# A hybrid decoder block on one core: scans with one SBUF operand, carries left in place, fused state and gate operations, ordered loads in the down stage

## The chip, the cores and the metric

The kernel runs on one core of a Trainium2 chip. The metric is the device time of one execution in microseconds (us). The time before is the median of three runs. The core's engines are TensorE (PE, matmuls and transposes; PEld is its weight load), VectorE (DVE), ScalarE (ACT), GpSimd (POOL) and SyncE (SP), whose queue issues most of the DMAs.

## The reference

One decoder layer for 2048 tokens of width 1024, in float32. A projection feeds three token mixers that work side by side:

```
q, k = rms_norm(q), rms_norm(k)                     # stick-breaking attention, 6 heads of 64
z = q @ k.T * scale                                 # keys s < query t only
A[t, s] = sigmoid(z[t, s]) * prod_{s<j<t} (1 - sigmoid(z[t, j]))
o_b = rms_norm(A @ v)                               # per head
S_t = diag(exp(log_f_t)) S_{t-1} + k_t^T v_t        # GLA (4 heads, 48 x 96), HGRN2 (4 heads, 128 x 64)
o_t = q_t S_t                                       # then rms_norm per head, times silu(gate)
x = x + concat(o_a, o_b, o_c) @ w_out               # the Out stage
gate, up = rms_norm(x) @ w_ffn_up                   # d_ff = 2816
x = x + (silu(gate) * up) @ w_ffn_down
```

The product over j is a running product from right to left, so 1 - sigmoid(z) = sigmoid(-z) is scanned along the keys from the newest to the oldest.

## The kernel before

The work runs in stages: projections (0 to 755 us of the trace), mixers (755 to 1592, from 1425 on mixed with the first tiles of Out), Out alone (1592 to 1782), the FFN's up half (to 2639) and its down half (to 3146). Matmuls in float32 are done as three matmuls on high and low parts (names ending in h and l): a high part is a rounding on ScalarE (L248), a low part a subtraction on DVE or POOL (L249). A scheduler puts the instructions of each engine, and the DMAs on SP's queue, in the order of an estimate of its own; `tc.keep_in_program_order` holds an instruction behind the one written before it on its engine or queue. In the mixers the order of PE is written out by hand (`Chain`).

**Stick-breaking.** A unit is one head, a group of 512 queries and a chunk of 512 keys: 60 units, each in four slots of 128 queries (`z_step`). A slot makes z (128 queries x up to 512 keys) in one of two PSUM banks, kp = sigmoid(-z) and w = sigmoid(z) on ScalarE into SBUF, then the scan on DVE (L993). The scan reads kp twice: as its data and as a second operand that the operation `bypass` ignores. Its result pr has one column more than keys; the leftmost, the product over the whole chunk, is copied by POOL into a carry tile (L996) for the next older chunk of the same head. Last, w times the shifted pr (L997), mostly on POOL. Then w is transposed by PE (`t_step`) and multiplied with v (`a_step`).

**The recurrences.** `hg_chunk` and `gla_chunk` update their states s_h and s_g 15 times each: POOL multiplies by the decay (L1192, L1247), DVE adds the new part from PSUM (L1193, L1248).

**Out.** Sixteen tiles of 128 tokens. `load` takes the mixers' output m, sums squares per head (14 ScalarE squares, L826), forms the inverse roots and multiplies m by them (three on DVE, L834) and by the gates (three on POOL). `turn` transposes m by PE into a PSUM bank (mt, L849) and splits it. 48 matmuls (po) a tile add the product with w_out. `norm` squares and scales the sum for the FFN (L857, L860); `left` transposes it through the same single bank (xt, L867) and copies it out (xa, L869), and `left_sums` stores operands of the seven products of a Strassen scheme to `xs_s`.

**Up.** `left_in` loads them and splits them into SBUF tiles (ah, al) that stay for all 22 steps of a half. These tiles' region on the right side of SBUF is that of Out's pools and of the output weights woh and wol, which close before.

**Down.** Seven products, in the order 1, 2, 5, 6, 3, 7, 4, each with 11 k's of 24 matmuls (8 PSUM banks, three matmuls each): 1848. For each k, `left_dn` loads one or two left tiles (ar, xa; 512 KB) from `hs_s`, which up has written, and `right_dn` weights (br, xb; 256 KB); products 5, 6, 3 and 4 go on from the tiles xa and xb of an earlier product. After the third k of product 1 the 16 tiles of acc (the residual) are loaded in program order. After a product `flush_dn` adds its eight banks to acc; for products 5 and 7 ScalarE copies the bank to tmp (L1528) and POOL adds that to a second part (L245). Finished parts of acc are stored to the output after products 2, 3, 7 and 4.

Of the kernel before, what the change touches and what calls it, by code (L numbers as in the profile page):

```python
# [14 lines left out]
ALU = mybir.AluOpType  # L15
# [47 lines left out]
def hybrid_block(ctx: ExitStack, tc: tile.TileContext, x, norm_mix_g, w_in, gla_w_decay,  # L63
# [740 lines left out]
    class Out:  # L804
        def open(self):
# [5 lines left out]
            self.pt = open_pool(self.st, "d_pt", 1, PSUM, side="right")  # L811

        def load(self, t):
# [15 lines left out]
            dve.tensor_scalar(ms[:, 4:14], ms[:, 4:14], 1.0 / SD, EPS, op0=ALU.mult,  # L829
                              op1=ALU.add)  # L830
# [13 lines left out]
        def turn(self, prep, hf):  # L844
            t, m, _, mh, ml = prep
            pt = self.pt.tile([P, 4, P], F32, tag="pt", name=f"mt{t}_{hf}")
# [15 lines left out]
        def left(self, t, xt, kh):  # L862

            pt = self.pt.tile([P, KH, P], F32, tag="pt", name=f"xt{t}_{kh}")
# [61 lines left out]
    with ExitStack() as ph:  # L926
# [16 lines left out]
        kps = [sbk.tile([P, 513], F32, name=f"kp{i}", bufs=1) for i in range(NKP)]  # L943
        for t_ in kps:
            pool.memset(t_[:, 512:513], 1.0)
# [13 lines left out]
        def z_step(u, b):  # L959
            h, g, c = u.h, u.g, u.c  # L960
            if b == 0:
                if u.diag:
                    u.q = sio.tile([P, 2, 512], F32, tag="sq", name=f"sq{h}_{g}", bufs=3)
                    for s in range(2):
# [3 lines left out]
                    u.carry = [sbk.tile([P, 1], F32, tag=f"ca{i}", name=f"ca{h}_{g}_{i}", bufs=4)  # L968
                               for i in range(4)]
                else:  # L970
                    p = units[u.i - 2]
                    u.q, u.carry = p.q, p.carry
# [22 lines left out]
            if c > 0:  # L995
                pool.tensor_copy(u.carry[b], pr[:, 0:1])  # L996
# [597 lines left out]
```

## Time and profile before

| | before |
|---|---|
| median of three runs | 3143.91 us (3139.87 to 3149.15) |
| profiled execution | 3147.62 us |
| span of its trace | 3145.8 us |
| PE busy | 2831.5 us (90%) |
| DVE busy | 2116.2 us (67%) |
| ACT busy | 1344.4 us (43%) |
| POOL busy | 1639.2 us (52%) |

The span goes from the first to the last instruction of the profiled execution. The busy shares are means over stages that differ in what limits them, so the windows by stage have to be read for each part of the change.

### The profile page before, as it was taken

How to read it: one execution, taken by the hardware profiler on the slowest of the kernel's cores; microseconds unless marked ns; L12 is line 12 of the kernel's file. 1: busy time of each engine (PE TensorE's matmuls, PEld its weight loads, DVE VectorE, ACT ScalarE, POOL GpSimd, SP SyncE). 2: the span in 40 equal slices, each digit the busy share in tenths (PEclk: the TensorE clock that was granted, in tenths of full speed). 3: DMA queues.
4: the chain of work that ended last, by engine and by line, in shares of the span. 5: the costliest groups of instructions: out<-in, count | busy, mean ns of one | idle time of the engine just before them, and what ended most of it. 6: DMA issues, size and time to landing. Idle time of an engine off the chain costs nothing. (4 is left out here: it accounts for less than half of the span.)

```text
span 3145.8 us, 43879 instructions
## 1 busy us (share of the span) xinstructions
PE 2831.5 (90%) x14882; PEld 2309.9 (73%) x14882; DVE 2116.2 (67%) x3508; ACT 1344.4 (43%) x2834; POOL 1639.2 (52%) x1640
## 2 busy tenths in 40 slices
PE   5898999997888889878888799999999997899998
PEld 5897878996666666655666588888788885677776
DVE  8886665886888888988866455555755553267443
ACT  5554534453555555566644333333433332323222
POOL 5342554344787887854633244444544442257635
PEclk9999999998889998989988899999999998999999
DMA  3534432536533333123354332222422225564173
GB/s 116 159 108 134 139 127 97 136 94 166 153 104 107 98 100 93 58 94 108 130 173 161 134 114 85 87 87 84 142 87 81 81 81 216 212 234 144 64 241 131
DMA packets 346095, 389.82 MB, mean 124 GB/s; under 512 B 59152, under 2 KB 258064, under 8 KB 344080
## 3 DMA queue, kind: packets, MB, share of 16 engines
q1 hardware_dynamic: 341776, 381.77, 38.4%
q0 software_dynamic: 4096, 5.25, 0.5%
q8 instruction: 119, 1.95, 0.3%
q14 instruction: 104, 0.85, 0.1%
HBM read 278.93 MB, written 108.00 MB: 123 GB/s over the span
## 5 line engine op out<-in xcount | busy, mean ns | idle before, releaser
L1390 PE MATMUL gu<-ah,uh 128*128 128x512 f32 x1232 | 481.3, 391 | 10.1 <-ACT ah L248 10.1
L1391 PE MATMUL gu<-al,uh 128*128 128x512 f32 x1232 | 481.8, 391 | 6.0 <-DVE al L249 5.9
L1392 PE MATMUL gu<-ah,ul 128*128 128x512 f32 x1232 | 481.0, 390 | 0.0
L249 POOL TENSOR_TENSOR ul<-bs,uh 128x512 fp32r<-128x512 f32 x176 | 241.6, 1374 | 243.2 <-ACT uh L248 243.2
L249 POOL TENSOR_TENSOR ul<-us,uh 128x512 fp32r<-128x512 f32 x132 | 176.6, 1339 | 203.6 <-ACT uh L248 203.6
L1390 PEld LDWEIGHTS gu<-ah,uh 128*128 128x128 f32 x1232 | 232.3, 189 | 60.3 <-ACT ah L248 12.0
L1391 PEld LDWEIGHTS gu<-al,uh 128*128 128x128 f32 x1232 | 232.5, 189 | 56.9 <-DVE al L249 8.7
L1552 PE MATMUL dn<-dbh,dah 128*128 128x512 f32 x616 | 224.6, 402 | 48.4 <-ACT dbh L248 41.8
L1392 PEld LDWEIGHTS gu<-ah,ul 128*128 128x128 f32 x1232 | 232.3, 189 | 48.1
L245 DVE TENSOR_TENSOR h<-h,gu 128x512 f32<-128x512 f32 x176 | 120.9, 687 | 205.3 <-PE gu L1392 123.5
L1553 PE MATMUL dn<-dbl,dah 128*128 128x512 f32 x616 | 243.9, 396 | 12.7 <-POOL dbl L249 12.6
L1554 PE MATMUL dn<-dbh,dal 128*128 128x512 f32 x616 | 242.4, 395 | 3.1 <-DVE dal L249 3.0
L248 ACT ACTIVATE uh<-bs 128x512 fp32r<-128x512 f32 x176 | 110.9, 632 | 299.8 <-PE gu L1391 299.6
L993 DVE TENSOR_TENSOR_SCAN pr<-kp,ca 128x513 f32<-128x513 f32 x144 | 213.2, 1484 | 22.0 <-ACT kp L990 17.7
L997 POOL TENSOR_TENSOR w<-w,pr 128x512 f32<-128x512 f32 (+1 forms) x174 | 191.8, 1102 | 46.0 <-DVE pr L993 26.0
L990 ACT ACTIVATE kp<-z 128x512 f32<-128x512 f32 (+1 forms) x240 | 128.0, 533 | 183.4 <-PE z L104 168.7
L104 PE MATMUL z<-sk,sq 128*128 128x512 f32 (+1 forms) x480 | 170.7, 440 | 14.5 <-ACT w L991 8.1
L107 PE MATMUL wt<-ident,w 128*128 128x128 f32 x816 | 147.9, 294 | 39.2 <-POOL w L997 34.3
L1552 PEld LDWEIGHTS dn<-dbh,dah 128*128 128x128 f32 x616 | 118.4, 194 | 80.5 <-ACT dbh L248 49.3
L249 DVE TENSOR_TENSOR dal<-ar,dah 128x1024 fp32r<-128x1024 f32 x44 | 65.0, 1485 | 163.1 <-ACT dah L248 163.0
L248 ACT ACTIVATE uh<-us 128x512 fp32r<-128x512 f32 x132 | 83.1, 631 | 193.0 <-PE gu L1391 130.6
L104 PEld LDWEIGHTS z<-sk,sq 128*128 128x128 f32 x480 | 80.7, 208 | 104.7 <-issue 37.9
(385 smaller groups left out, 7845.1 us busy)
## 6 DMA issues: line engine op xcount, KB each, us to landing
us<-in_w_ffn_up SPq DMA_DIRECT2D x88, 512.0 KB, 3.8
ar<-hs_s SPq DMA_DIRECT2D x88, 512.0 KB, 4.0
hs_s<-h SPq DMA_DIRECT2D x44, 512.0 KB, 2.6
br<-in_w_ffn_down SPq DMA_DIRECT2D x88, 256.0 KB, 3.2
sk<-sk_s SPq DMA_DIRECT2D x60, 256.0 KB, 2.9
st<-xs_s SPq DMA_DIRECT2D x14, 1024.0 KB, 5.2
xt<-in_x SPq DMA_DIRECT2D x24, 512.0 KB, 4.8
sq<-sq_s SPq DMA_DIRECT2D x48, 256.0 KB, 4.8
```

What stands on the lines that cost most here:

```text
L104: self._add(nc.tensor.matmul(*a, **k))
L107: self._add(nc.tensor.transpose(*a, **k))
L248: act.activation(wh, st, AF.Copy)
L249: eng.tensor_tensor(wl, st, wh.bitcast(F32), op=ALU.subtract)
L993: dve.tensor_tensor_scan(pr[:, n::-1], kr, kr, 1.0 if u.diag else u.carry[b], op0=ALU.mult, op1=ALU.bypass)
L997: (dve if (b in DVE_B0 if g == 0 else b == DVE_B) else pool).tensor_tensor(w, w, pr[:, 1:n + 1], op=ALU.mult)
L1390: pe.matmul(pv, bh[:, k, :], ah[:, :, k, :], start=(k == 0), stop=False)
L1391: pe.matmul(pv, bh[:, k, :], al[:, :, k, :], start=False, stop=False)
L1392: pe.matmul(pv, bl[:, k, :], ah[:, :, k, :], start=False, stop=(k == KH - 1))
L1552: pe.matmul(pss[i], ah[:, ts_], bh, start=(k == 0), stop=False)
L1553: pe.matmul(pss[i], ah[:, ts_], bl, start=False, stop=False)
L1554: pe.matmul(pss[i], al[:, ts_], bh, start=False, stop=(k == NK - 1))
```

## The change

1. `z_step`: the scan's second operand, which `bypass` ignores, is a broadcast column of z in PSUM in place of kp. The results pr go to two fixed buffers of 529 columns, each slot at an offset `at` of its own, so that the leftmost column stays unharmed until the next chunk reads it as its carry; the POOL copies go. Where DVE multiplies, the second sigmoid is written over z in PSUM, and the product reads it there.
2. `hg_chunk`, `gla_chunk`: a multiplication and an addition become four, or two, fused operations on DVE that read the new part from PSUM.
3. `Out.load`: one ScalarE square of the whole tile and three DVE sums replace 14 squares; 14 fused DVE products replace three products on DVE and three on POOL.
4. Out has three more PSUM banks for its transposes once the mixers have closed theirs.
5. Up: the ah and al tiles of the first half are allocated in the reversed order of the products.
6. Down: all loads in program order, raw weight tiles in three buffers, the products in the order 1, 5, 6, 2, 3, 7, 4, both additions of products 5 and 7 by DVE from PSUM, and product 6's 16 POOL additions put off, two to each k of the next product.

```diff
@@ Out.load
+            sq = self.wk.tile([P, D], F32, tag="sq", name=f"msq{t}", bufs=1)
+            act.activation(sq, m, AF.Square)
             for a, b, w, i, j in segs:
-                for h in range(j - i):
-                    sj = self.sm.tile([P, GDV], BF16, tag="sj", name=f"sj{t}_{i}_{h}", bufs=1)
-                    act.activation(sj[:, :w], m[:, a + h * w:a + (h + 1) * w], AF.Square,
-                                   accum_out=ms[:, i + h:i + h + 1])
+                dve.tensor_reduce(ms[:, i:j], sq[:, a:b].rearrange("p (h d) -> p h d", d=w),
+                                  axis=AX.X, op=ALU.add)
...
             for a, b, w, i, j in segs:
-                mv = m[:, a:b].rearrange("p (h d) -> p h d", d=w)
-                dve.tensor_tensor(mv, mv, rs[:, i:j].unsqueeze(2).to_broadcast([P, j - i, w]),
-                                  op=ALU.mult)
-            pool.tensor_tensor(m[:, 0:384], m[:, 0:384], gt[:, 0:384], op=ALU.mult)
-            pool.tensor_tensor(m[:, 768:], m[:, 768:], gt[:, 384:], op=ALU.mult)
-            mv = m[:, 384:768].rearrange("p (h d) -> p h d", d=SD)
-            pool.tensor_tensor(mv, mv, gs64.unsqueeze(1).to_broadcast([P, SH, SD]), op=ALU.mult)
+                for n in range(i, j):
+                    cs = slice(a + (n - i) * w, a + (n - i + 1) * w)
+                    g_ = gt[:, cs] if a == 0 else gs64 if a == 384 else \
+                        gt[:, 384 + (n - i) * w:384 + (n - i + 1) * w]
+                    dve.scalar_tensor_tensor(m[:, cs], m[:, cs], rs[:, n:n + 1], g_,
+                                             op0=ALU.mult, op1=ALU.mult)
@@ z_step
-            pr = sbk.tile([P, 513], F32, tag="pr", name=f"pr{h}_{g}_{c}_{b}")
+            at = 4 * (g - c) + 2 * u.j + b // 2
+            pr = prs[b % 2][:, at:at + 513]
             act.activation(kp[:, :n], z, AF.Sigmoid, scale=-1.0)
-            act.activation(w, z, AF.Sigmoid)
             kr = kp[:, n::-1] if n < 512 else kp[:, ::-1]
-            dve.tensor_tensor_scan(pr[:, n::-1], kr, kr, 1.0 if u.diag else u.carry[b],
-                                   op0=ALU.mult, op1=ALU.bypass)
-            if c > 0:
-                pool.tensor_copy(u.carry[b], pr[:, 0:1])
-            (dve if (b in DVE_B0 if g == 0 else b == DVE_B) else pool).tensor_tensor(w, w, pr[:, 1:n + 1], op=ALU.mult)
+            on_dve = b in DVE_B0 if g == 0 else b == DVE_B
+            act.activation(z if on_dve else w, z, AF.Sigmoid)
+            dve.tensor_tensor_scan(pr[:, n::-1], kr, z[:, 0:1].to_broadcast([P, n + 1]),
+                                   u.carry[b], op0=ALU.mult, op1=ALU.bypass)
+            u.last.append(pr[:, 0:1])
+            if on_dve:
+                dve.tensor_tensor(w, z, pr[:, 1:n + 1], op=ALU.mult)
+            else:
+                pool.tensor_tensor(w, w, pr[:, 1:n + 1], op=ALU.mult)
@@ hg_chunk (gla_chunk: the same with two)
-            pool.tensor_tensor(s_new, s_old, dec.to_broadcast([P, HH, HDV]), op=ALU.mult)
-            dve.tensor_tensor(s_new, s_new, pu, op=ALU.add)
+            for i in range(HH):
+                dve.scalar_tensor_tensor(s_new[:, i, :], s_old[:, i, :], dec[:, i, :], pu[:, i, :],
+                                         op0=ALU.mult, op1=ALU.add)
@@ between Out and up
+    out_.ptx = open_pool(ptx, "d_px", 3, PSUM)
     for t in outs:
         pass
...
+    ops = {m: tuple(hp.tile([P, 4, KH, P], F32R, tag=f"{x}{m}", name=f"{x}{m}_0")
+                    for x in ("ah", "al")) for m in ORDER[::-1]}
     tiles = {m: left_in(0, m, 4 if m == 1 else 2) for m in ORDER}
@@ down
     def load_a(t_, k, j, kh):
-        dma.dma_start(t_, hs_s[kh * NK + k][j].rearrange("p i j t -> p (i j t)"))
+        tc.keep_in_program_order(
+            dma.dma_start(t_, hs_s[kh * NK + k][j].rearrange("p i j t -> p (i j t)")))
...
-        dma.dma_start(t_, w_dn[r:r + P, j * 512:j * 512 + 512])
+        tc.keep_in_program_order(dma.dma_start(t_, w_dn[r:r + P, j * 512:j * 512 + 512]))
...
         elif m in (5, 7):
             c = {5: c12, 7: c21}[m]
-            tmp = rop.tile([P, 512], F32, tag="tmp", name=f"tmp{m}_{i}")
-            act.activation(tmp, ps, AF.Copy)
             add(c, c, ps)
-            add(c22, c22, tmp, pool)
+            add(c22, c22, ps)
...
         elif m == 6:
             u = held[i]
             add(u, u, ps)
-            add(c12, c12, u, pool)
             add(c21, c21, u)
-            add(c22, c22, u, pool)
+            later.append(lambda: add(c12, c12, u, pool))
+            later.append(lambda: add(c22, c22, u, pool))
...
-    for m in (1, 2, 5, 6, 3, 7, 4):
+    for m in (1, 5, 6, 2, 3, 7, 4):
...
+            for fn in later[:2]:
+                fn()
+            del later[:2]
```

## Rows read from the trace of the kernel before

**Rows 1.** The page's head.
```profile
span 3145.8 us, 43879 instructions
```
**Rows 2.** Windows: length, busy PE, PEld, DVE, ACT, POOL, clock, DMA share, GB/s.
```profile
755.00:1425.00 670.00, 576.83 (x4024) 435.04 (x4025) 565.29 (x904) 372.41 (x938) 517.44 (x762) 0.90 0.38 109
1592.00:1782.00 190.00, 148.66 (x641) 116.14 (x640) 112.27 (x315) 71.73 (x265) 59.91 (x51) 0.86 0.48 158
1812.00:2209.00 397.00, 397.00 (x1752) 328.83 (x1753) 234.28 (x273) 132.70 (x213) 196.38 (x146) 1.00 0.28 91
2645.00:2650.00 5.00, 0.00 (x0) 0.00 (x0) 0.00 (x0) 0.00 (x0) 0.00 (x0) 0.50 1.02 408
```
**Rows 3.** Groups by line, mixers: busy us, mean ns, idle before and what ended it.
```profile
L993 DVE TENSOR_TENSOR_SCAN pr<-kp,ca 128x513 f32<-128x513 f32 x144 | 213.2, 1484 | 22.0 <-ACT kp L990 17.7 <-POOL w L997 1.7 <-ACT sj L826 1.1
...
L997 POOL TENSOR_TENSOR w<-w,pr 128x512 f32<-128x512 f32 x132 | 159.7, 1210 | 41.9 <-DVE pr L993 21.9 <-ACT w L991 15.2 <-ACT wth L1007 1.9
...
L996 POOL COPY ca<-pr 128x1 f32<-128x1 f32 x144 | 45.1, 314 | 85.3 <-DVE pr L993 56.6 <-DVE rfy L84 9.2 <-DVE rmy L84 4.5
```
**Rows 4.** Single lines: shortest, median, longest ns; the scans' idle time before them.
```profile
L993 DVE TENSOR_TENSOR_SCAN pr<-kp,ca x144: 1247/1286/2356, 856.2 to 1569.7; 128x513 f32<-128x513 f32 x144
...
  ACT kp L990: 69.3, 49
...
L245 DVE TENSOR_TENSOR chf<-chf,phf x28: 673/687/689, 293.6 to 495.2; 128x512 f32<-128x512 f32 x28
...
L84 DVE SCALAR_TENSOR_TENSOR rmy<-rma,rmy x48: 147/174/1246, 1411.0 to 1721.8; 128x14 f32<-128x14 f32 x48
...
L1193 DVE TENSOR_TENSOR s_h<-s_h,hpu x15: 387/390/408, 823.9 to 1371.7; 128x256 f32<-128x256 f32 x15
```
**Rows 5.** Timeline of one attention slot: start, us, engine, line, operation.
```profile
1106.49 0.73 PE L104 MATMUL z<-sk,sq 128*128 128x512 f32 x2
...
1107.26 0.60 ACT L990 ACTIVATE kp<-z 128x512 f32<-128x512 f32 x1 [3.21 <-PE z L104]
...
1107.75 0.59 ACT L991 ACTIVATE w<-z 128x512 f32<-128x512 f32 x1
```
**Rows 6.** Groups by line, Out's preparation on DVE.
```profile
L834 DVE TENSOR_TENSOR m<-m,rmy 128x256 f32<-128x256 f32 x16 | 18.8, 1178 | 0.0
...
L834 DVE TENSOR_TENSOR m<-m,rmy 128x384 f32<-128x384 f32 x32 | 16.6, 554 | 0.5
```
**Rows 7.** Timeline of Out, two groups of transposes on PE.
```profile
1737.05 0.60 PE L867 MATMUL xt<-ident,xt 128*128 128x128 f32 x4
...
1738.38 0.66 PE L849 MATMUL mt<-ident,m 128*128 128x128 f32 x4 [0.74 <-ACT xa L869]
```
**Rows 8.** Chain of waits, the same step of tiles three apart (two lie between).
```profile
1721.92 1.15 ACT mh L857 x2
...
1769.46 1.15 ACT mh L857 x2
```
**Rows 9.** Timeline of ACT and of PE at the start of up.
```profile
1784.11 4.08 ACT L248 ACTIVATE ah<-st 128x512 fp32r<-128x512 f32 x6 [6.21 <-DMA xs_s<-xs]
...
1784.79 0.79 PE L1390 MATMUL gu<-ah,uh 128*128 128x512 f32 x1 [7.53 <-ACT ah L248]
```
**Rows 10.** Timeline at the start of down: SP's last store, PE's two long waits.
```profile
2641.15 0.32 SPq L1418 DMA_DIRECT2D hs_s<-h  x1
...
2662.54 3.44 PE L1552 MATMUL dn<-dbh,dah 128*128 128x512 f32 x8 [23.53 <-ACT dbh L248]
...
2693.27 3.43 PE L1552 MATMUL dn<-dbh,dah 128*128 128x512 f32 x8 [12.75 <-ACT dbh L248]
```
**Rows 11.** Groups by line, down stage.
```profile
L248 ACT ACTIVATE dah<-ar 128x1024 fp32r<-128x1024 f32 x44 | 46.3, 1056 | 114.3 <-PE dn L1553 105.7 <-DVE ar L242 8.6
...
L245 DVE TENSOR_TENSOR acc<-acc,dn 128x512 f32<-128x512 f32 x48 | 31.4, 681 | 28.1 <-ACT tmp L1528 18.6 <-PE dn L1554 9.5
...
L242 DVE TENSOR_TENSOR xa<-ar,xa 128x1024 f32<-128x1024 f32 x11 | 20.3, 1853 | 0.2
```
**Rows 12.** The page's DMA issues: KB each, median us from issue to landing.
```profile
ar<-hs_s SPq DMA_DIRECT2D x88, 512.0 KB, 4.0
```

More of the change, by code (lines that the diff above doesn't have):

```diff
@@ L811, in open, with pt_tile @@
             self.pt = open_pool(self.st, "d_pt", 1, PSUM, side="right")
+            self.ptx = None
+        def pt_tile(self, name):
+            return (self.ptx or self.pt).tile([P, KH, P], F32, tag="pt", name=name)
         def load(self, t):
@@ L845, in turn @@
             t, m, _, mh, ml = prep
-            pt = self.pt.tile([P, 4, P], F32, tag="pt", name=f"mt{t}_{hf}")
+            pt = self.pt_tile(f"mt{t}_{hf}")
             for j in range(4):
@@ L862, in left @@
         def left(self, t, xt, kh):
-            pt = self.pt.tile([P, KH, P], F32, tag="pt", name=f"xt{t}_{kh}")
+            pt = self.pt_tile(f"xt{t}_{kh}")
             for j in range(KH):
@@ L943, in hybrid_block @@
         kps = [sbk.tile([P, 513], F32, name=f"kp{i}", bufs=1) for i in range(NKP)]
+        prs = [sbk.tile([P, 513 + 16], F32, name=f"pr{i}", bufs=1) for i in range(2)]
         for t_ in kps:
@@ L967, in z_step @@
                                       .rearrange("j p t -> p j t"))
-                    u.carry = [sbk.tile([P, 1], F32, tag=f"ca{i}", name=f"ca{h}_{g}_{i}", bufs=4)
-                               for i in range(4)]
+                    u.carry = [1.0] * 4
                 else:
                     p = units[u.i - 2]
-                    u.q, u.carry = p.q, p.carry
+                    u.q, u.carry = p.q, p.last
+                u.last = []
                 k = sio.tile([P, 512], F32, tag="sk", name=f"sk{h}_{g}_{c}")
@@ L1246, in gla_chunk @@
             s_new = rec.tile([P, 2, GDV], F32, tag="s_g", name=f"s_g_{c}", bufs=2)
-            pool.tensor_tensor(s_new, s_old, dec.to_broadcast([P, 2, GDV]), op=ALU.mult)
-            dve.tensor_tensor(s_new, s_new, pu, op=ALU.add)
+            for i in range(2):
+                dve.scalar_tensor_tensor(s_new[:, i, :], s_old[:, i, :], dec[:, i, :], pu[:, i, :],
+                                         op0=ALU.mult, op1=ALU.add)
             state["g"] = s_new
@@ L1371, in left_in @@
         st = stp.tile([P, 4, KH, P], F32, tag="st", name=f"st{ip}_{m}")
-        hi, lo = (hp.tile([P, 4, KH, P], F32R, tag=f"{x}{m}", name=f"{x}{m}_{ip}")
-                  for x in ("ah", "al"))
+        hi, lo = (ops[m] if ip == 0 else
+                  (hp.tile([P, 4, KH, P], F32R, tag=f"{x}{m}", name=f"{x}{m}_{ip}")
+                   for x in ("ah", "al")))
         dma.dma_start(st, xs_s[ip][m])
@@ L1445, in hybrid_block @@
     lop = open_pool(pd, "g_lo", 3, side="right")
+    bop = open_pool(pd, "g_bo", 3, side="right")
     lrp = open_pool(pd, "g_lr", 1, side="right")
     accp = open_pool(pd, "g_acc", 1)
-    rop = open_pool(pd, "g_ro", 2)
+    rop = open_pool(pd, "g_ro", 1)
     psd = open_pool(pd, "g_psd", 8, PSUM)
@@ L1490, in raw @@
         def raw(kh, j):
-            t_ = rop.tile([P, 512], F32, tag="br", name=f"br{nm}_{kh}{j}")
+            t_ = bop.tile([P, 512], F32, tag="br", name=f"br{nm}_{kh}{j}")
             load_b(t_, k, kh, j)
@@ L1513, in right_dn, with done @@
         return hi, lo
-    held = {}
+    held, later = {}, []
+    def done(t, hf):
+        cs = slice(hf * 512, hf * 512 + 512)
+        dma.dma_start(out[t * P:(t + 1) * P, cs], acc[t][:, cs])
     def flush_dn(m, i, ps):
@@ L1521, in flush_dn @@
         if m == 1:
-            u = held[i] = rop.tile([P, 512], F32, name=f"u{i}", bufs=1)
+            u = held[i] = rop.tile([P, 512], F32, name=f"u{i}")
             act.activation(u, ps, AF.Copy)
@@ L1539, in flush_dn @@
             add(c, c, ps)
-        done = {2: (i, 0), 3: (i, 1), 7: (8 + i, 1), 4: (8 + i, 0)}.get(m)
-        if done is not None:
-            t, hf = done
-            cs = slice(hf * 512, hf * 512 + 512)
-            dma.dma_start(out[t * P:(t + 1) * P, cs], acc[t][:, cs])
-    for m in (1, 2, 5, 6, 3, 7, 4):
+            done(*{2: (i, 0), 3: (i, 1), 4: (8 + i, 0)}[m])
+    for m in (1, 5, 6, 2, 3, 7, 4):
         pss = [psd.tile([P, 512], F32, tag="dn", name=f"dn{m}_{i}") for i in range(8)]
@@ L1559, in hybrid_block @@
                     acc.append(a)
+            for fn in later[:2]:
+                fn()
+            del later[:2]
         for i in range(8):
             flush_dn(m, i, pss[i])
+    for fn in later:
+        fn()
     pd.close()
```

11 lines of the change are left out of this document (7 added, 4 removed).

## Prediction

> **What bounds the kernel now.** I read the page's head first: the profiled execution spans 3145.8 us [rows 1]; it took 3147.62 us (1.8 around the span), 3.7 over the median of 3143.91. Differences under some 9 us (0.3%) I count as no change, about what a measurement of this kernel tells. Next the windows by stage, because the change touches five stages with different limits. In the FFN up TensorE is busy all the time, 397.00 of 397.00 us for 1752 matmuls, or 0.2266 us each [rows 2]; only its start can gain. In the mixers PE works 576.83 of 670 us, but VectorE 565.29 and POOL 517.44 [rows 2]: three engines nearly full, with an order written by hand, so no one of them alone is the bound. In the Out stage PE is busy 148.66 of 190 us at a granted clock of 0.86 [rows 2]. Then came the groups by line, the scan's own durations and waits, the timeline of one attention slot, the chain of waits in Out, and the timeline at the three stage borders.
>
> **The scan and the carries (mixers, 755 to 1592).** The 144 scans that take a carry average 1.484 us [rows 3], while their shortest is 1.247 and their median, over the same form, 1.286 [rows 4]. I put the difference down to POOL: the longest takes 2.356 [rows 4], and DVE's chf additions, at a time when POOL leaves them alone, hold 0.673 to 0.689 [rows 4]. With the PSUM operand I let the mean fall to the median: 144 x 0.198 = 28.5 us of DVE time, and at most 144 x 0.237 = 34. What that operand itself costs is not in the trace for a scan; for an addition of 128x512 it is nothing, 0.681 with PSUM [rows 11] against 0.687 [rows 4]. 144 carry copies leave POOL: 45.1 us [rows 3]. POOL's 132 wide products average 1.210 [rows 3]; if they lose the other side of the contention, say a tenth, POOL gains some 16 us more.
>
> The Trainium skill, "SBUF — State Buffer", section "Who interferes with whom", says that a VectorE instruction with two SBUF inputs contends with a GpSimd instruction that reads SBUF, and one with at most one SBUF input (outside its two-port modes) does not. The trace agrees as far as it goes (0.689 at most beside a quiet POOL, 2.356 in the mixers [rows 4]); by the rule the 28.5 us are the right size, and without it they would be 0.
>
> Against that stand two new waits. The scan now reads the bank of z, which ScalarE still reads for its second sigmoid; where DVE takes the product, that sigmoid even writes into z. So I let every scan wait for the second sigmoid, 0.59 us after the first (0.60) [rows 5]. The evidence is a wait of the same kind: DVE's acc additions sat 18.6 us for ScalarE's copy out of the same bank [rows 11]. It costs where DVE had been idle for the first sigmoid: 49 times, 69.3 us in all [rows 4], so 49 x 0.59 = 29 us; elsewhere DVE comes late anyway. Behind a waiting scan stand the recurrences' gates and Out's norms on DVE, and PE's transposes of w wait for it. Second, z's two banks are held until the scan ends. One bank's round is then z 0.73, the two sigmoids 1.19, the scan 1.29 (and 0.69 for a product on DVE), 3.2 to 3.9 us with hardly a queue; two banks serve two slots, and a slot (60 units of four) has (1570 - 755)/240 = 3.4 us, so 6.8 us are there. It fits with some 3 us for queues.
>
> The PSUM bank rule speaks against the change: the Trainium skill, "PSUM — Partial Sum Buffer", section "PSUM bank collisions raise a hardware error", wants two engines kept out of one bank by semaphores. The trace agrees as far as one wait can, with 18.6 us [rows 11]. By it the 29 us are paid in full; without it the mixers would gain them.
>
> The states: six small fused operations for each of 15 chunks take the place of two DVE additions and two POOL products. A fused operation of 14 columns has a median of 0.174 us, the addition of 256 columns 0.390 [rows 4]; between them a column costs 0.9 ns, so 64 to 96 columns are 0.22 to 0.25, say 0.23. With both additions at 0.39: 15 x (6 x 0.23 - 0.78) = +9 us on DVE, POOL freed.
>
> On DVE: -28.5 + 9 and a wait of +29; on POOL -61 and the two products. The three engines are equally full, so I give the mixers little: **-8 us**, a tenth of POOL's relief and no more than the DVE balance spoils. Bounds: -45 (POOL's copies in full, no new wait) and +70.
>
> **The Out stage (1592 to 1782).** The two marks of one ScalarE line, 1721.92 and 1769.46, lie three tiles apart [rows 8]: 15.85 us a tile. PE needs 48 x 0.2266 = 10.9 and four groups of four transposes at 0.60 to 0.66 [rows 7], 2.5: 13.4. The excess sits where PE waits for the one transpose bank, 0.74 us for ScalarE's copy [rows 7], several times a tile, and in the clock of 0.86 that follows. With three more banks this goes. ScalarE loses 14 squares a tile for one square. DVE becomes the rival: 112.27/10 = 11.2 us a tile now [rows 2]; out go 2 x 0.554 + 1.178 = 2.3 [rows 6], in come 14 fused products (0.23 as above, POOL's own products gone from beside them: 3.2) and three sums over 1024 columns (by the addition's 0.68 per 512 columns [rows 11], 1.4): 13.5. Two engines that both need 13.4 to 13.5 leave some idle time between them; I take 13.8: (15.85 - 13.8) x 10 = **-20 us**. Bounds 0 (DVE at 15.8) and -31 (PE alone, with shorter transposes). POOL's products go; nobody waits for POOL there.
>
> **Out to up.** PE starts the up stage at 1784.79, when ScalarE has the first operand; ScalarE started at 1784.11 after 6.21 us of waiting for the xs stores [rows 9]. These had to leave the region that product 1's tiles overlay. In reversed order these tiles lie over the output weights, free when the last po matmul is done, near 1769 (the mark before it is 1769.46 [rows 8]). Product 1's data are those of the first eight tiles, stored long ago. A load by 4 us [rows 12] and a copy put the start at 1772 to 1775, but PE still has two groups of transposes of the last tile to do, which wait for its norm: **-11 us**, bounds -3 and -13.
>
> **The down stage (2639 to the end).** 1848 matmuls at 0.2266 are 419 us of 507: 88 us to spare. Two stalls are named: 23.53 before the first matmul and 12.75 before k = 3 [rows 10].
> - Start. The last store of h is issued at 2641.15 [rows 10]. Behind it the scheduler had put loads in its own order, and with the loads at 408 GB/s [rows 2] the first pair came late. Program order loads the first operand at once: 2641.5 + 4.0 [rows 12] + 1.06 for its rounding [rows 11] = 2646.7, and the wait is 8.1 instead of 23.5: -15.4.
> - k = 3. The 16 acc loads (8.4 MB) now stand between k = 2 and k = 3 behind 2.4 MB: 10.8 MB at 408 GB/s is 26.4 us from 2641.5, 0.8 MB more 1.9, the rounding 1.1: 2671-2673. PE has done three k's at some 2664.6 (2646.7 + 3 x 24 x 0.2266 = 2663, restart 1.6). Stall 8.7: -4.
> - Then the order costs something. The loads of products 3, 7 and 4 stand on SP's queue behind the eight stores of products 2, 3 and 7, and the eighth store waits for the last flush. So nothing is loaded ahead there. A border costs the flush 0.68 [rows 11], the store's issue 0.32 [rows 10], the landing 4.0 [rows 12], the operand's subtraction 1.85 and its rounding 1.06 [rows 11]: 7.9 us. Where POOL must subtract and make the low half, two steps of 1.2 [rows 3] or more behind other POOL work, up to 12. I take 9.6, and 1.6 for the restart (eight matmuls took 3.43 us instead of 1.81 [rows 10]; 8 x 0.2266 = 1.81): 3 x 11.2 = +33.6.
> - Against it, of the 88 us 48 are left without the two stalls and their restarts (36.3 + 3.2): short waits for POOL's and DVE's operands and flushes. With deferred additions, no ScalarE copies and three raw buffers I leave 16 of them (POOL then has, in a k of product 2, a low half and two deferred additions, 3.6 us at 1.2 each [rows 3] and 5 at the worst, of the 24 x 0.2266 = 5.4 that PE takes; it fits, but barely), the tail of some 5 among them: -32.
>
> In all -15.4 - 4 + 33.6 - 32 = -17.8, **-17 us**; bounds -50 (the borders cost nothing) and +10 (borders at 14, the short waits stay half).
>
> Sum: -8 - 20 - 11 - 17 = -56, span 3089.8, with 1.8 around it 3091.6; less the 3.7 by which the profiled run lies above the median, **3088 us**.
>
> **The rivals.** (A) POOL was the mixers' limit, and its relief arrives: -45 there, not -8: 3051. For it speak POOL's 517 us and that 41.9 us of its idle time before w ended with the scan [rows 3]; against it that the scan itself comes later. (B) The borders in the down stage cost nothing, as DMA runs ahead after all: 33.6 less: 3054. For it speaks that a landing takes only 4.0 us [rows 12]; against it the stores' place in SP's queue. (C), the other side: the z loop becomes the bound. If each of the 240 scans starts 0.6 us late because its second sigmoid is late, and z's bank with it, that is 144 us less 61 to 68 of relief: +76 in place of -8, so 3172. It decides once a slot loses more than 48/240 = 0.2 us net, as much as the other three stages give. For it: DVE is busy 84% and queues in front of the scan; against it the 3 us of slack in the round.
>
> **How the numbers follow.** Forecast 0.50, with a range of its own of 3055 to 3115; A 0.20, B 0.14, C 0.16. Range 3025 to 3145: it takes in A and B, leaves out C above 3145 (0.11) and A with B together (0.05). Faster: A, B and 0.46 of the forecast's 0.50: 0.80; same: 0.04 of it and 0.04 of C, 0.08; slower: the rest of C, 0.12.
>
> **What would show it.** Scans' mean near 1.29 with a maximum below 1.5 shows the contention right; idle time before the scan ended by the second sigmoid, the new wait. Out tiles 13.4 to 14 us apart; first up matmul by 1776; first down matmul near 2647 less what came before; holes of 8 to 12 us at three product borders. A hole-free border means B, a longer stretch from 755 to 1592 means C, and there z matmuls that wait for the scan. The prediction fails if the fused Out products cost well over 0.3 us or the mixers lose 50 us.

## The result and the profile after

The changed kernel took 3166.09 us (median of 4 runs, 3162.43 to 3173.27) beside 3143.78 for the kernel before on the same chip: ratio 1.0073, interval 1.0049 to 1.0096. It is slower by 0.7%; forecast were 3088 us, a range to 3145 and 12 in 100 for slower. In the experiments below, a time is the median of several runs and a ratio is that to the kernel before timed beside them; 0.001 is 3.1 us. The kernel before took 3143.78 us beside the changed kernel and 3149.58 to 3151.36 beside the experiments, so a gain over the changed kernel comes out 5 to 11 us larger by the ratios, which the text gives, than by the times. "From first to last scan" and the like are read from the starts that the trace gives for a line, in one profiled execution of each kernel.

The page's head after, then windows of the mixers and of Out alone (length, busy PE, PEld, DVE, ACT, POOL, clock, DMA share, GB/s):

```profile
span 3164.4 us, 43263 instructions
```
```profile
753.00:1420.00 667.00, 570.53 (x3976) 434.78 (x3976) 517.16 (x930) 354.11 (x845) 370.60 (x604) 0.90 0.38 108
...
1620.00:1800.00 180.00, 143.28 (x645) 114.68 (x643) 124.68 (x417) 44.92 (x76) 34.45 (x26) 0.88 0.50 163
```

Against [rows 2] POOL fell from 517 to 371 us in the mixers, and the stage still grew: POOL's time was not what it lacked. DVE's 517 in place of 565 comes mostly from the window, in which the slower kernel gets less done: from first to last scan DVE works 663 us in place of 689. In Out ScalarE and POOL have emptied, while DVE rose to 125 of 180 us. Next the scans, and the matmuls of Out, up and down (shortest, median, longest ns; first and last start):

```profile
L998 DVE TENSOR_TENSOR_SCAN pr<-kp,pr,z x144: 1241/1272/1285, 855.3 to 1601.0; 128x513 f32<-128x513 f32 x144
...
L906 PE MATMUL po<-woh,ml x160: 387/389/797, 1622.0 to 1794.9; 128*128 128x512 f32 x160
...
L1403 PE MATMUL gu<-ah,uh x1232: 387/389/796, 1804.1 to 2662.3; 128*128 128x512 f32 x176
...
L1569 PE MATMUL dn<-dbh,dah x616: 388/389/796, 2666.0 to 3159.4; 128*128 128x512 f32 x154
```

The kernel before has its last scan at 1569.7 [rows 4] and these starts of its matmuls (the first scans, of narrower tiles, start at 756.0 before and 754.9 after):

```profile
L904 PE MATMUL po<-woh,ml x160: 387/390/776, 1591.5 to 1768.1; 128*128 128x512 f32 x160
...
L1390 PE MATMUL gu<-ah,uh x1232: 388/389/792, 1784.8 to 2638.2; 128*128 128x512 f32 x176
...
L1552 PE MATMUL dn<-dbh,dah x616: 387/389/796, 2662.5 to 3140.8; 128*128 128x512 f32 x154
```

Laid side by side, they give the whole balance of the span:

| stretch | before | after | difference | forecast |
|---|---|---|---|---|
| start to first scan | 756.0 | 754.9 | -1.1 | 0 |
| first to last scan (mixers) | 813.7 | 846.1 | +32.4 | -8 |
| last scan to last po (Out) | 198.4 | 193.9 | -4.5 | -20 |
| last po to first up matmul | 16.7 | 9.2 | -7.5 | -11 |
| up | 853.4 | 858.2 | +4.8 | 0 |
| last up to first down matmul | 24.3 | 3.7 | -20.6 | -15.4 |
| down, first to last | 478.3 | 493.4 | +15.1 | -2 |
| end | 5.0 | 5.0 | 0 | |
| span | 3145.8 | 3164.4 | +18.6 | -56 |

**Mixers.** Who waited for whom (engine, line, releaser: us in total, times, longest):

```profile
POOL w L1004 <- DVE pr L998: 208.5, 122, 7.6
PEld z L104 <- DVE pr L998: 73.3, 32, 7.4
PE z L104 <- DVE pr L998: 46.0, 25, 5.3
...
DVE pr L998 <- ACT z L997: 41.2, 19, 6.4
...
DVE pr L998 <- ACT w L997: 26.7, 21, 4.1
...
PE z L104 <- DVE w L1002: 22.2, 17, 3.0
```

PE now waits 46 + 22 us for z's bank until DVE's scan or product is done; before, nothing on DVE held that bank. (PEld's wait is for the same z, beside PE's.) The scans wait 41 + 27 us for the second sigmoid, nearly the 69.3 they had waited for the first [rows 4]. And POOL, relieved, waits 208.5 us for scans. PE's waiting time in all grows less than these waits: from first to last scan it is 846.1 - 716.1 = 130 us in place of 813.7 - 703.9 = 110, because waits of other kinds became shorter. Of the 32 us, 20 are waiting and 12 longer work. One case of the wait for the bank in the timeline (start, us):

```profile
1210.73 0.59 ACT L997 ACTIVATE z<-z 128x512 f32<-128x512 f32 x1
...
1214.13 1.27 DVE L998 TENSOR_TENSOR_SCAN pr<-kp,pr,z 128x513 f32<-128x513 f32 x1
1215.51 0.69 DVE L1002 TENSOR_TENSOR w<-z,pr 128x512 f32<-128x512 f32 x1
...
1216.25 1.22 PE L104 MATMUL z<-sk,sq 128*128 128x512 f32 x2 [3.04 <-DVE w L1002]
```

The sigmoid is done at 1211.3. DVE has the recurrences' work in front until 1214.13, then scan and product, and PE gets the bank at 1216.2, after a stand of 3.04 us, and starts slowly (1.22 us where 0.73 was usual [rows 5]).

**The borders of the down stage.** SP's queue at the first border, PE there and at the second and third:

```profile
2934.98 5.09 SPq L1536 DMA_DIRECT2D out<-acc  x8
2940.16 0.40 SPq L1471 DMA_DIRECT2D ar<-hs_s  x1
```
```profile
2947.63 3.78 PE L1569 MATMUL dn<-dbh,dah 128*128 128x512 f32 x8 [8.64 <-ACT dah L248]
...
3021.03 3.35 PE L1569 MATMUL dn<-dbh,dah 128*128 128x512 f32 x7 [10.62 <-ACT dbh L248]
...
3097.22 3.78 PE L1569 MATMUL dn<-dbh,dah 128*128 128x512 f32 x8 [13.89 <-ACT dbh L248]
```

Eight stores, then the first load: 8.64 + 10.62 + 13.89 = 33.2 us.

### The profile page after: what moved, and what is told of

It reads as the page before. It is cut to its first block, busy times and chain, and to the rows that moved or that the text cites. A ratio compares the mean times of both kernels' runs of the same rounds, so it can differ in the third digit from the quotient of the medians.

```text
span 3164.4 us, 43263 instructions
## 1 busy us (share of the span) xinstructions
PE 2836.1 (90%) x14882; PEld 2321.6 (73%) x14882; DVE 2115.8 (67%) x3808; ACT 1282.6 (41%) x2386; POOL 1423.3 (45%) x1402
## 4 chain that ended last, share of the span: by engine, by line
PE 56%; DVE 16%; DMA 5%; issue 5%; POOL 2%; ACT 2%; SPq 1%; DVEq 0%; POOLq 0%; ACTq 0%
PE gu L1404 9%; PE gu L1405 9%; PE gu L1403 8%; PE dn L1569 4%; DVE pr L998 4%; PE dn L1570 4%; PE dn L1571 3%; PE z L104 3%; PE av L104 2%; PE sch L104 2%; PE wt L107 2%; DVE m L840 1%; PE po L104 1%; PE scg L104 1%; DVE hq L1078 1%
## 5 line engine op out<-in xcount | busy, mean ns | idle before, releaser
L1004 POOL TENSOR_TENSOR w<-w,pr 128x512 f32<-128x512 f32 (+1 forms) x174 | 194.6, 1119 | 279.3 <-DVE pr L998 208.5
L1569 PE MATMUL dn<-dbh,dah 128*128 128x512 f32 x616 | 232.5, 407 | 52.3 <-ACT dbh L248 38.9
L1404 PEld LDWEIGHTS gu<-al,uh 128*128 128x128 f32 x1232 | 232.2, 188 | 61.5 <-DVE al L249 13.5
L104 PEld LDWEIGHTS z<-sk,sq 128*128 128x128 f32 x480 | 82.6, 213 | 180.5 <-DVE pr L998 73.3
L998 DVE TENSOR_TENSOR_SCAN pr<-kp,pr,z 128x513 f32<-128x513 f32 x144 | 182.1, 1271 | 20.4 <-ACT w L997 12.6
```

Of the source, the lines that this page charges most:

```text
L104: self._add(nc.tensor.matmul(*a, **k))
L998: dve.tensor_tensor_scan(pr[:, n::-1], kr, z[:, 0:1].to_broadcast([P, n + 1]), u.carry[b], op0=ALU.mult, op1=ALU.bypass)
L1004: pool.tensor_tensor(w, w, pr[:, 1:n + 1], op=ALU.mult)
L1404: pe.matmul(pv, bh[:, k, :], al[:, :, k, :], start=False, stop=False)
L1569: pe.matmul(pss[i], ah[:, ts_], bh, start=(k == 0), stop=False)
```

## The experiments

Theory 1: z's bank, held for DVE, costs the mixers' 32 us, and the ordered loads cost the borders. Rivals: the fused operations cost it, or the scheduler's other order. "Freed" below is the kernel of run 1, which several runs start from.

**1. z freed: both operands back in SBUF, carries still in place.**
```diff
-act.activation(z if on_dve else w, z, AF.Sigmoid)
+act.activation(w, z, AF.Sigmoid)
-... kr, z[:, 0:1].to_broadcast([P, n + 1]), ...
+... kr, kr, ...
-dve.tensor_tensor(w, z, pr[:, 1:n + 1], op=ALU.mult)
+dve.tensor_tensor(w, w, pr[:, 1:n + 1], op=ALU.mult)
```


> The changed kernel with one part undone: the scan's second operand is kp in SBUF again, the second sigmoid always goes to w in SBUF, and DVE's products read w there; the carries stay in the scans' buffers. Theory 1 (the bank of z, held until the scan or DVE's product is done, makes PE's next z wait): PE's waits for the scan and for DVE's product before z, 175 us counted on both of its queues in the changed kernel, go away; the scans get their contention back (mean near 1.45 us in place of 1.27, 28 us of DVE time); the last scan starts by 1575 in place of 1601 and the whole takes 3130 to 3142. Theory 2 (the small fused state operations, or the missing POOL copies through another order of the scheduler, cost the 32 us): the last scan stays at 1600 or later and the whole at 3160 to 3180, since contention is added. Theory 3 (contention was the larger evil): over 3180.

Measured: 3134.49 us, ratio 0.9939 (0.9919 to 0.9960): 0.0134 or 42 us better than the changed kernel. Its last scan starts at 1566.4, 810.5 after the first. By the times it is 32 us, by the mixers' length 36. So the two operands in z's bank, with the order of instructions that comes with them, cost the mixers their loss. The contention came back (longest scan 2.309) without harm:

```profile
L998 DVE TENSOR_TENSOR_SCAN pr<-kp,pr x144: 1246/1281/2309, 857.6 to 1566.4; 128x513 f32<-128x513 f32 x144
```

**2. Only the product's operand back in SBUF** (the first and third edit of run 1).

> The changed kernel, but where DVE takes the product the second sigmoid goes to w in SBUF and the product reads it there; the scan still reads the broadcast column of z in PSUM. Of the two holders of z's bank only the scan is left. If the scan's hold is the price (PE waited 119 us for the scan, counted on both queues, and 56 for the product), about two thirds of what the run with both undone gives stay lost: last scan at 1590 to 1596, whole 3156 to 3164. If the product's hold and its in-place sigmoid are the price (the scan waits 41 us for it): last scan near 1575, whole 3135 to 3145.

Measured: 3141.51, 0.9970 (0.9954 to 0.9985), last scan 1567.7. On this path three quarters of run 1's gain (32 of 42 us) come from the 66 slots whose product DVE takes, and 9 from the scan's own operand; run 5 will split it otherwise. PE still waits for z's bank behind the scans, longer than in the changed kernel (46.0), and yet the mixers take 812.7 us, no more than before the change:

```profile
PE z L104 <- DVE pr L998: 52.6, 44, 3.6
```

So this wait does not by itself cost the stage its time.

**3. The hold alone, added to run 2.**
```diff
 dve.tensor_tensor(w, w, pr[:, 1:n + 1], op=ALU.mult)
+dve.tensor_copy(junk, z[:, 0:1])
```


> The run with the product's operand in SBUF (3141, last scan at 1568), plus one thing: after each of the 66 products on DVE, DVE copies one column of z to a scratch tile, so z's bank is held until then as in the changed kernel (the copies are 66 x 0.15 = 10 us of DVE time at most). If the hold is the cause, the last scan comes at 1592 or later and the whole takes 3160 or more, as the changed kernel. If it isn't, the last scan comes by 1576 and the whole takes 3140 to 3150.

Measured: 3144.53, 0.9987 (0.9973 to 1.0001): 5 us more than run 2, which the two intervals don't separate, and the time of the case in which the hold isn't the cause. The last scan, at 1583.9, lies between the cases; of the 13 us by which the mixers are longer than in run 2, 10 are longer work of PE, at a granted clock of 0.90 in place of 0.92, and 3 are waiting. The hold until DVE's product alone does not explain the loss.

**4. In DVE's slots the scan reads kp; sigmoid and product stay in z's bank.**
```diff
-... kr, z[:, 0:1].to_broadcast([P, n + 1]), ...
+... kr, kr if on_dve else z[:, 0:1].to_broadcast([P, n + 1]), ...
```


> The changed kernel, but in the slots where DVE takes the product the scan's second operand is kp in SBUF, so the scan does not wait for the sigmoid that is written over z; that sigmoid and the product stay in z's bank, held as before. If the hold is the cause: last scan at 1592 or later, whole 3158 to 3172. If the scan's wait for the sigmoid in place (41 us in 19 waits in the changed kernel) is the cause: last scan by 1577, whole 3140 to 3148.

Measured: 3159.39, 1.0029 (1.0011 to 1.0047): 14 us back, and a time of the first case. The last scan, at 1583.0, fits neither case, but the profiled execution was the quickest of ten (3147.99): the granted clock of its mixers was 0.93 in place of 0.90, and PE waits there for 130 us, as in the changed kernel. The run shows the contention within one kernel, scans of 513 columns with z and with kp:

```profile
L998 DVE TENSOR_TENSOR_SCAN pr<-kp,pr,z x108: 1232/1272/1284, 852.3 to 1583.0; 128x513 f32<-128x513 f32 x108
...
L998 DVE TENSOR_TENSOR_SCAN pr<-kp,pr x36: 1240/1276/2347, 846.9 to 1564.6; 128x513 f32<-128x513 f32 x36
```

**5. Both operands of DVE's slots in SBUF, POOL's slots as changed** (runs 2 and 4 together).

> The changed kernel with both operands of the slots whose product DVE takes back in SBUF (scan from kp, product from w); only POOL's slots scan with z's column. From first to last scan the three other cases took 846 us (both in z), 828 (product in z alone) and 813 (scan's operand in z alone). If the hold and the wait are two separate prices of 16 to 18 us and 13 to 20 us, this case takes 793 to 800 and the whole 3118 to 3130. If they cost only together (the bank held long because the scan is late), it takes 808 to 816 and the whole 3134 to 3145.

Measured: 3163.34, 1.0038 (1.0022 to 1.0054), past both cases: 11 us back by the ratios, 3 by the times. The mixers take 851.7 us in the profiled execution, the slowest of nine (3180.05), at a granted clock of 0.89. PE's waits for z on DVE are all but gone, and another has come, the transposes' for POOL's products:

```profile
PEld wt L107 <- POOL w L1004: 70.3, 36, 6.7
...
PE wt L107 <- POOL w L1004: 61.6, 35, 6.5
...
PE z L104 <- ACT w L997: 12.7, 17, 4.3
...
PE z L104 <- DVE pr L998: 5.5, 7, 1.7
```

As an account by waits theory 1 falls here: PE's waits for the banks are gone, and most of the lost time stays. Run 1 differs from this run only in the scans of POOL's slots, which read kp there and z's column here. This one operand is worth 1.0038 - 0.9939, 31 us, where run 2 against run 1 left 9 us for the operand of all scans. So the gains of single operands don't add, and no split of the 42 us holds.

**6 and 7. A third bank for z while the recurrences run, taken from their scores; beside it the control with the bank taken away alone.**

> The changed kernel as it was timed, with a third bank for z while the recurrences run; their own scores and updates have two banks in place of three for it. If two banks held until DVE's scan or product ends are what costs the 32 us, the third takes PE's waits for z's banks down to a third or less, and the last scan starts 20 to 35 us earlier than in the run with two banks for z and two for the recurrences (which is the one to compare with). If the price is the scan's own wait for the second sigmoid, written in place, or DVE's load, a third bank changes the last scan by less than 8 us.

> The changed kernel with two banks in place of three for the recurrences and nothing given to z: what the lost bank costs by itself. Between 0 and 30 us more than the changed kernel (3166 to 3196); the run with a third bank for z is read against this one.

Measured: 3183.37, 1.0108 (1.0082 to 1.0133), against 3189.36, 1.0131 (1.0107 to 1.0155). Last scans 1623.1 and 1628.2: 5 us for a third bank, not clear of the intervals. PE's waits for z's bank did fall, to a fifth, first with the third bank and then in the control:

```profile
PE z L104 <- DVE pr L1000: 6.5, 5, 3.2
...
PE z L104 <- DVE w L1004: 4.2, 2, 2.4
```
```profile
PE z L104 <- DVE pr L998: 37.2, 18, 4.4
...
PE z L104 <- DVE w L1002: 13.9, 11, 2.7
```

40 us of waits gone and 5 us gained, which is the second case: the number of banks is not what the loss hangs on. kp has two buffers as well, which the scan frees; whether that ring binds next was not tried.

The runs on the mixers side by side (us from first to last scan; waiting is the length less PE's busy time):

| run | ratio | length | PE busy | PE waiting | granted clock |
|---|---|---|---|---|---|
| before | 1 | 813.7 | 703.9 | 109.8 | 0.91 |
| changed | 1.0073 | 846.1 | 716.1 | 130.0 | 0.90 |
| 1, both operands in SBUF | 0.9939 | 810.5 | 704.5 | 106.0 | 0.91 |
| 2, only the scan's in z's bank | 0.9970 | 812.7 | 706.8 | 105.9 | 0.92 |
| 3, as 2, bank held | 0.9987 | 826.0 | 716.7 | 109.3 | 0.90 |
| 4, as changed, DVE's slots scan from kp | 1.0029 | 828.4 | 698.2 | 130.2 | 0.93 |
| 5, 2 and 4 together | 1.0038 | 851.7 | 729.1 | 122.6 | 0.89 |
| 6, third bank for z | 1.0108 | 865.4 | 730.2 | 135.2 | 0.89 |
| 7, control of 6 | 1.0131 | 870.5 | 734.3 | 136.2 | 0.89 |

Runs 1 to 3, in which the second sigmoid isn't written over z, wait as little as the kernel before; run 4, in which it is, waits as long as the changed kernel. Run 5 doesn't fit this. What speaks for the scheduler's order as a part of the cause is that DVE's order is another in each form: run 8's first kernel, which leaves the mixers alone, has all 1313 DVE instructions of the stage in the changed kernel's order, as far as names and shapes tell; runs 2, 4, 5 and 1 have some 1150, 1110, 1015 and 850 of them in it.

**8. Only product 1's loads ordered in the down stage.**
```diff
-tc.keep_in_program_order(dma.dma_start(...))
+d = dma.dma_start(...)
+if pinned[0]: tc.keep_in_program_order(d)
 for m in (1, 5, 6, 2, 3, 7, 4):
+    pinned[0] = m == 1
```


> The changed kernel, with only product 1's loads of the down stage in program order; those of the other six products may be put ahead by the scheduler. If the loads queued behind the stores make the three holes (8.8, 10.8 and 14.1 us between products, with a slow restart of 1.6 to 2 us each), the three holes shrink to under 3 us each and the whole takes 3127 to 3137. If the operands' own chains on POOL, DVE and ACT make the holes, they stay above 6 us each and the whole takes 3155 to 3166. A third way: the loads put ahead take buffers from the product under way, and stalls inside the products rise by 10 us or more, as in the kernel before.

> Both together: z's bank freed after the second sigmoid (operands back in SBUF) and only product 1's loads in program order. If the two losses are independent and both theories hold, the gains add: 3166 less 25 to 35 less 30 to 38, so 3095 to 3112. If one theory falls, it equals the run of the other one alone, within 5 us.

Measured: 3159.64, 1.0025 (1.0008 to 1.0041); together with run 1, 3122.89, 0.9910 (0.9886 to 0.9935). The third way happened, and the two gains together are 3123 in place of the 3095 to 3112 said. SP's queue and PE in the second of the two:

```profile
2634.69 10.49 SPq L1471 DMA_DIRECT2D xa<-hs_s  x9
2646.19 21.00 SPq L1580 DMA_DIRECT2D acc<-x_s  x16
2668.21 0.32 SPq L1471 DMA_DIRECT2D ar<-hs_s  x1
```
```profile
2680.13 3.78 PE L1574 MATMUL dn<-dbh,dah 128*128 128x512 f32 x8 [22.30 <-ACT dbh L248]
```

Product 5's xa tiles, which wait for no buffer, went ahead of product 1's fourth left tile.

**9. Products 1, 5, 6 and 2 ordered, 3, 7 and 4 free** (`pinned[0] = m in (1, 5, 6, 2)`, on the freed kernel).

> The kernel with z's bank freed early, and in the down stage the loads of products 1, 5, 6 and 2 in program order, those of 3, 7 and 4 free. In the run with only product 1 ordered, nine xa loads and then the acc loads went ahead of product 1's fourth left tile (a hole of 22.3 us at k = 3 instead of 11 to 13) while the three holes at the product borders shrank to 2.6 us and less. If it was product 5's xa that did the harm, ordering it keeps both gains: hole at k = 3 of 11 to 14, borders under 4 us, first down matmul by 4 us after the last of up, whole 3092 to 3106. If loads of products 3, 7 and 4 can do the same harm, a new hole over 8 us shows in products 1 to 2 and the whole is 3115 to 3135.

Measured: 3103.63, 0.9868 (0.9849 to 0.9888), 0.0071 or 22 us under run 1; down takes 465.4 us from first to last matmul in place of 493. The three holes at the borders are 2 us and less, with one of 4.2 inside the last product's first k. The order of the first four products is worth keeping, that of the last three cost some 22 to 28 us.

**10. The deferred additions one to a k** (`later[:1]`, on run 9).

> The same with product 6's 16 deferred POOL additions put one to a k (over products 2 and 3) in place of two. If their clump (nine additions of 1.3 to 1.9 us around the low half of product 2's third k) makes the holes of 6.2 and 2 us at the start of product 2, these go: 6 to 9 us less than the run with two to a k. If the scheduler draws the additions together anyway, or the low half is late for another reason, no change within 3 us.

Measured: 3109.57, 0.9886 (0.9863 to 0.9909): no gain. The hole, 6.0 us in the trace, stayed at its place; what it depends on was not found.

**11 to 13. Out on the freed kernel: one transpose bank again; the whole preparation of `load` as before; only the products as before (square and three sums kept).**

> The kernel with z's bank freed early, without the three additional transpose banks. If the one bank had set Out's 15.85 us a tile, the eight tiles from the ninth po to the sixteenth take 147 us or more again in place of 139 (8 us or more lost), and the whole takes 3142 or more. If Out hangs on something else (the chain of DVE's products, the loads of m, the stores of x2 that the scaling waits for), they take 139 to 142 and the whole 3130 to 3138.

> The kernel with z's bank freed early, with Out's preparation as before the change (14 squares on ScalarE, three products on DVE, three on POOL), the three banks kept. If the 14 fused DVE products are the new chain that eats the gain of the banks, Out gets faster: eight tiles in 130 or less in place of 139, whole 3122 to 3128. If ScalarE's squares and POOL's products were the limit, they take 146 to 150 again, whole 3140 to 3146. If neither, within 3 us of 3134.

> The kernel with z's bank freed early; in Out's preparation the square of the whole tile and the three sums stay, but the 14 fused DVE products are again three products on DVE and three on POOL. With the whole old preparation 23 us were gained (3134 to 3111). If the fused products were what cost them (4.2 us of DVE a tile by the trace of the changed kernel, 0.28 to 0.46 each, in place of 2.2), this run gains as much: 3108 to 3116. If it was the square and the sums (1.07 and 1.5 us in a row behind m's load), it stays at 3130 to 3137. Half and half: 3119 to 3126.

Measured: 3143.32, 0.9990 (0.9971 to 1.0008); 3111.34, 0.9895 (0.9870 to 0.9920); 3116.24, 0.9892 (0.9868 to 0.9916). From last scan to last po: 213.2, 180.5 and 174.2 us, against 198.0 in run 1. So in the stage the banks gain 15 us and the fused products lose 24 (by the ratios of the whole 16 and 15; run 13's profiled execution was the quickest of four); the square and the sums cost nothing that shows. In the changed kernel's chain of waits the fused products stand in front of a tile's low part, and PE restarts behind it:

```profile
1678.03 6.10 DVE m L840 x13
1684.20 0.61 DVE ml L90
1684.85 0.80 PE po L906
```

**14. The three repairs together** (run 1, the old preparation, run 9).

> The three repairs together: z's bank freed early, Out's preparation as before the change, loads of products 3, 7 and 4 free. If their gains are independent: 3104 less 20 to 26, so 3076 to 3086, 0.977 to 0.981 of the kernel before. If part of them overlaps (DVE's relief in Out only moved the mixers' tail), 3090 to 3100.

Measured: 3084.83, 0.9797 (0.9773 to 0.9820), 2% under the kernel before; the gains add. The mixers take 801.3 us.

**15 to 17. On the repaired kernel: the old states; the scan's operand in z again; up's tiles in the old order.**

> The repaired kernel (3085) with the states as before the change: the decay's product on POOL, one addition on DVE. If DVE is what the mixers lack, giving POOL 29 us and taking 9 or more from DVE ends the mixers 3 to 10 us earlier, whole 3075 to 3082. If POOL's missing products helped more (the recurrence's chain is shorter by a hand-over of two engines), 3088 to 3100. If both are off the path, within 3 us of 3085.

> The repaired kernel (3085) with the scan's second operand in z's bank again, the second sigmoid and the product in SBUF. Beside each other the two forms had taken 3134 and 3141. If the contention relief (28 us of DVE) and the scan's wait with the bank's hold cancel: 3082 to 3094. If the relief is worth more now that DVE is freed in Out: under 3080. If the hold weighs more: over 3096.

> The repaired kernel (3085) with up's first tiles allocated in the order of the products, as before the change. If the reversed order gains what the kernel before lost there (first up matmul 16.7 us after Out's last po matmul, against 9.3 in the repaired kernel), up starts 6 to 9 us later and the whole takes 3088 to 3094. In the changed kernel up took 4.8 us longer after its early start (waiting for the second product's load); if that gives the gain back, the whole is within 3 us of 3085.

Measured: 3104.56, 0.9858 (0.9840 to 0.9877); 3098.21, 0.9844 (0.9818 to 0.9870); 3083.88, 0.9794 (0.9771 to 0.9817). The fused states gain 19 us (mixers 825.1 without, 801.3 and, in run 17, 807.5 with them), a little past the case that was said for them. The scan's operand costs 15 (mixers 819.0). In the mixers run 15 differs from the kernel before by the carries alone, left in place without POOL's copies, and it takes 825.1 us where that takes 813.7. It is one execution of each, so no price; but no gain shows from the 45 us of copies that POOL was spared. The order of the tiles is worth nothing: with the old one up starts 16.1 us after the last po instead of 9.3, and takes 5.4 us less.

## Why the prediction was wrong

**The mixers' sum (-8; +32.4 came).** The failing step is "It fits with some 3 us for queues", by which z's bank, shared with DVE, stands in the sum at nothing. Run 1 shows that the two operands in that bank cost 42 us. The round of the bank counted the work, 3.2 to 3.9 us, and took the rest for slack; in the case shown DVE's queue had 2.8 us of the recurrences' work between a sigmoid and its scan, nearly the whole slack. So the sign that was named for the rival on the other side, C, came: z matmuls that wait for DVE, and a longer stage. C's price was +76; the stage lost 32.4/240 = 0.14 us a slot.

By which wait the 42 us come is open. The wait for the bank shows the place and not the price: run 2 has as much of it as the changed kernel and no loss, and the third bank took 40 us of it away for 5 us. The hold alone gave 5 us (run 3), DVE's slots scanning from kp 14 (run 4), both operands freed in DVE's slots 11 (run 5), the scan's operand 9, 15 or 31 by the kernel around it (run 2 against 1, run 16, run 5 against 1). The wait moves: PE's idle time ahead of z (waits for loads left out) falls from 81 us in the changed kernel to 18 in run 5, and that ahead of wt, the transposes of w, rises from 15 to 58. An order held fixed by hand while only the operand changes would tell; it wasn't tried.

**Contention (28.5 us of DVE): right, and worth little.** The scans' longest fell from 2.356 to 1.285 and their median hardly moved [rows 4]. 144 x (1.484 - 1.271) = 31 us of DVE were saved. That POOL is the other side shows in the kernel before: of its 144 scans the 28 that no POOL instruction overlaps take 1.287 us at most, the other 116 1.534 on average; after the change 75 overlap one and none is over 1.285. In this the Trainium skill's page "SBUF — State Buffer", section "Who interferes with whom", holds: run 4 has both kinds side by side, 1.284 us at most with z's column and 2.347 with kp. The prediction's own evidence was misread: POOL did not leave the chf additions alone, it worked beside 19 of the 28; they stay at 0.689 us and less with one operand in SBUF and one, phf, in PSUM. POOL did not gain the 16 us said for its side: its wide products take 1.216 us after, 1.210 before [rows 3]. DVE's saving was not won as time. The wait for the second sigmoid took the place of the one for the first, 68 us for 69; it was not 29 more.

**The states (+9 us of DVE): counted as a cost, they were a gain.** DVE's time for them rose by 14 us (25.3 for 10.9; 0.27 and 0.30 us an operation, where 0.23 was said), and still the fused form gains 19 us on the repaired kernel (run 15). The sum counted DVE's time and not the chain from one chunk to the next, which loses a hand-over between two engines. That this is the reason is not shown; only the size is.

**Out (-20; -4.5).** The banks were right: 15 us (run 11). The step that failed took the fused products as DVE's time alone, 13.5 us a tile, with "nobody waits for POOL there". The fused products cost 4.2 us a tile, not 3.2 (0.28 to 0.46 each in the trace, not 0.23), and they stand in one queue with the low parts and the sums that PE waits for, where POOL had worked beside it. Run 13 prices that at 24 us in the stage, 15 in the whole. The 15.85 us a tile, too, were those of the last three tiles only [rows 8]: over all ten tiles of Out alone the last po matmuls lie 17.9 us apart before (1589.3 to 1768.1) and 17.5 after (1619.8 to 1794.9). The last three alone came as forecast, 13.4 us apart.

**Out to up (-11; -7.5, and up longer by 4.8).** The start moved as said (1804.1, 9.2 after the last po). What followed was not in the step: the second product's load is not there yet, and PE waits again.

```profile
1809.90 5.99 DMA st<-xs_s
1815.91 1.07 ACT ah L248
1817.00 1.24 DVE al L249
1818.29 0.80 PE gu L1404
```

Run 17 nets it to zero.

**Down (-17; -5.5).** The borders were forecast at three times 9.6 us and a restart; they are 8.6, 10.6 and 13.9, and the restart takes 3.78 us for eight matmuls instead of 1.81: 33.2 + 3 x 2 = 39, not 33.6, and run 9 confirms the mechanism (rival B's premise, loads that run ahead, holds only when the order is taken off). The start was better than forecast, since the first pairs are loaded before h's last store: 3.7 us. The k = 3 stall stayed at 11.4 (8.7 said, where its own sum gives 6.4 to 8.4). The most mis-sized term is "short waits": 48 us to 16 was said. From first to last matmul 15.1 us were added: 39 at the borders, less 1.3 at k = 3, which by subtraction leaves 23 that the short waits gave, not 32.

## What to carry to other kernels

An operand moved into a buffer that another engine refills has a price that the durations of the work don't show; count the queue of the last reader as well. A wait that appears names the place and not the price: here waits for z's bank could be taken away for 5 us of gain, or kept without loss. Compare the whole waiting time of the bound engine, undo the edit, and remember that a scheduler gives another order with each form. Work taken from an idle engine and given to another is judged by the queue that the bound engine waits for, not by busy time: in Out the products that POOL gave to DVE cost 15 us, in the mixers the ones of the states gained 19. An order for loads is needed where free loads would run ahead of urgent ones (products 1 and 5), and hurts where the loads are put behind stores that wait for results (products 3, 7 and 4).

## What the runs showed that was not expected

Fusing two products on POOL and two additions on DVE into six small DVE operations a chunk gains 19 us in a stage in which DVE is busy 573 of 645 us. Taking a bank of three from the recurrences costs 1.0131 - 1.0073 = 0.006, 18 us (23 by the times). The parts of the change that are worth keeping make a kernel 2% faster than the one before (run 14), so the loss was not the idea as a whole but three of its parts.
